# A sixth gather buffer, and value tiles in the weights' ring, in a hybrid decoder step on one core

## The chip, the cores and the metric

The kernel runs on one core of one Trainium2 chip. The metric is the device time of one execution in microseconds (us); smaller is better. A core has TensorE (PE) for matrix products, VectorE (DVE), ScalarE (ACT) and GpSimd (POOL), and a queue of SyncE (SP) from which most DMAs are issued. Each engine runs its own instructions in order and waits on semaphores for the others.

## What is computed

One inference step of a two-layer decoder for 512 prompt tokens and 8 sampled tokens. Layer 0 is a chunked gMLP, layer 1 differential attention over shared keys and values. After each of them comes a PEER layer: 8 heads pick 16 of 16384 experts for every token.

```python
def peer_block(h, w_q, keys, u_tab, v_tab):
    q = (h @ w_q).reshape(T, PEER_HEADS, 2, PEER_QDIM // 2)
    s = jnp.einsum('thcd,hcnd->thcn', q, keys)
    sv, si = lax.top_k(s, PEER_TOPK)
    cand = sv[:, :, 0, :, None] + sv[:, :, 1, None, :]
    ...
    eidx = ...                                   # 128 experts for a token
    g = jax.nn.softmax(top_s, axis=-1)
    act = jax.nn.gelu(jnp.einsum('thkd,td->thk', u_tab[eidx], h))
    return jnp.einsum('thk,thkd->td', (g * act), v_tab[eidx])
```

Tables u and v have 16384 rows of 1024 float32 in each layer. The prompt is four tiles of 128 tokens (0 to 3); the sampled tokens are tile 4.

## The kernel before

In each layer two of the four prompt tiles get their experts by gathers and two by dense products over the whole tables (`DT`: tiles 0 and 1 dense in layer 0, tiles 2 and 3 in layer 1).

**Gathers** (`peer_tile`, lines 710 to 723): for each tile 128 rows of u and 128 of v for every token, each by an indirect DMA from POOL (`gather`, line 706) that brings 128 rows of 1024 float32 into a buffer of the pool `gb`, which has 5. DVE then multiplies a gathered u row tile by the tokens and sums (line 715), or adds a weighted v row tile to the residual x (line 722). There are 512 gathers in a layer. They need little else and are laid beside the rest of the kernel: `pins` and `anchors` allow each of these DVE operations only behind a certain instruction of the other work (`tick`).

**Dense experts** (`dense_peer`): the 128 blocks of 128 experts are done in four quarters q of 32 blocks il. `acts(q)` loads a tile of u (`ub`, line 483, 512 KB) from the ring `wt`, which the pool `wp` keeps with 4 buffers for all weights. In quarter 0 it is multiplied by float32 matmuls (line 494). In the others `split` makes a high part (ACT, line 209) and a low part (DVE, line 211), with two buffers each, and 24 matmuls follow (lines 488, 489, 491); ACT writes the gelu into `W[q]`. `gates(q)` builds one-hot tiles (ACT, lines 526 and 529, or DVE, line 520), multiplies them on PE (line 533) and applies the gates to `W[q]`. The value loop (lines 552 to 586) loads a tile of v (`vb`, line 561, 512 KB) for each block and accumulates W x v into four PSUM banks (line 576, or with split operands in quarter 3, lines 572 to 574).

In program order, quarter 0's activations come first, then quarter 0's gates with quarter 1's activations. In the value loop of quarter q each of the first four value tiles (`NV` = 4) is followed by 8 activations of quarter q + 1, where those aren't done yet (q = 1 and 2); the other 28 are interleaved with the gates of quarter q + 1. Value tiles of quarter 3 come from the ring `wt`, all others from a ring `vb` of three in the pool `dpa`. The Tile framework orders the instructions of each engine when it compiles: an instruction that comes first in the program goes first if what it needs, a buffer among it, is free by then; otherwise later ones pass it.

**Fronts**: ahead of the dense experts of each layer stand the gMLP or the attention, for two groups of tiles, and `peer_front`, which makes queries and scores (ACT copies a score tile, line 650) and has DVE pick the top 16 (`topk_rank`). For the first group of a layer the scores go to a ring `s_k` of two in the pool `wk`, for the second to memory of its own (`sall`), and for the sampled tokens to `s_k` again (line 680).

Of the kernel before, what the change touches and what calls it, by code (L numbers as in the profile page):

```python
# [8 lines left out]
F32 = mybir.dt.float32  # L9
# [9 lines left out]
D = 1024  # L19
# [16 lines left out]
def body(ctx: ExitStack, tc: tile.TileContext, a):  # L36
# [1 line left out]
    V, SC, PE, GP, SY = nc.vector, nc.scalar, nc.tensor, nc.gpsimd, nc.sync  # L38

    per = ctx.enter_context(tc.tile_pool(name="per", bufs=1))  # L40
    gb = ctx.enter_context(tc.tile_pool(name="gb", bufs=5))
    ks = ctx.enter_context(tc.tile_pool(name="ks", bufs=2))
    wp = ctx.enter_context(tc.tile_pool(name="wp", bufs=4))
    pt = ctx.enter_context(tc.tile_pool(name="pt", bufs=4, space=bass.MemoryType.PSUM))
# [43 lines left out]
    def step(k=1):  # L88
        while k and bg:
            try:  # L90
                next(bg[0])
                k -= 1
            except StopIteration:
                bg.pop(0)
# [48 lines left out]
    def bcast_row(src, n, name, bufs=2, p=128):  # L143
        t = wk.tile([128, n], F32, name=name, tag="tmp" if n == D else f"bc{n}", bufs=1)
        SY.dma_start(t[:p], bass.AP(tensor=src.tensor, offset=src.offset, ap=[[0, p], [1, n]]))
        return t
# [60 lines left out]
    def split(w, k=1):  # L207
        wh = wp.tile([128, 8, 128], FR, name="wh", tag="wh", bufs=2)
        SC.activation(wh, w, AF.Copy)  # L209
        wl = wp.tile([128, 8, 128], FR, name="wl", tag="wl", bufs=2)  # L210
        tick(V.tensor_tensor(wl, w, wh.bitcast(F32), op=OP.subtract), k)  # L211
        return wh, wl
# [256 lines left out]
    def dense_peer(layer, dpa, open_rest, open_odd, smp):  # L469
# [3 lines left out]
        NQ, QI, NV = 4, 32, 4  # L473
# [78 lines left out]
        for q in range(NQ):  # L552
            na, ng = (na if not q else acts(q + 1), gates(q + 1)) if q + 1 < NQ else (iter(()), iter(()))
            for il in range(QI):
                i = q * QI + il
                w = W[q][:, il, :]
                r0 = layer * NE + i * 128
                three = q in V3[layer] and (il >= NV or q == NQ - 1)
                v = wp.tile([128, D], F32, name="vb", tag="wt") if three else \
                    dpa.tile([128, D], F32, name="vb", tag="vb", bufs=3)  # L560
                SY.dma_start(v, a["peer_v"][r0:r0 + 128, :])
                if three:
                    vh, vl = [z.rearrange("p c e -> p (c e)") for z in split(v.rearrange("p (c e) -> p c e", c=8), 0)]
                    wh = dpb.tile([128, 256], FR, name="wdh", tag="ohj", bufs=4)
                    SC.activation(wh, w, AF.Copy)
                    wl = dpb.tile([128, 256], FR, name="wdl", tag="ohj", bufs=4)
                    V.tensor_tensor(wl, w, wh.bitcast(F32), op=OP.subtract)
                for t in range(2):
                    for hf in range(2):
                        ts, hs = slice(t * 128, (t + 1) * 128), slice(hf * 512, (hf + 1) * 512)  # L570
                        if three:
                            PE.matmul(y[t][hf], wh[:, ts], vh[:, hs], start=i == 0, stop=False)
                            PE.matmul(y[t][hf], wh[:, ts], vl[:, hs], start=False, stop=False)  # L573
                            PE.matmul(y[t][hf], wl[:, ts], vh[:, hs], start=False, stop=i == 127)
                        else:
                            PE.matmul(y[t][hf], w[:, ts], v[:, hs], start=i == 0, stop=i == 127)  # L576
                if i == 2:
                    bg.append(peer_sample(layer, dpa, *smp))
                if il % 2 == 0:
                    step(1)  # L580
                if il < NV:
                    for _ in range(QI // NV):
                        next(na, None)
                else:
                    for _ in range((il - NV + 1) * 16 // (QI - NV) - (il - NV) * 16 // (QI - NV)):
                        next(ng, None)
# [5 lines left out]
    def peer_front(tiles, n, layer, ph):  # L592
        if any(t == 4 or t not in DT[layer] for t in tiles):
            gbc = bcast_row(a["f_norm_g"][layer], D, f"g_f{layer}")
        hT = dd["hT"] = full_T("hT")
        st = {}
        for t, r in zip(tiles, rms([(x[t], rows[t]) for t in tiles], D)):
            p = rows[t]
            if t < 4 and t not in DT[layer]:
                h = ks.tile([128, D], F32, name="h_g", tag="hg")  # L600
            elif t == 4:
                hs = ks.tile([128, D], FR, name="h_s", tag="hs", bufs=1)
                h = wa.tile([128, D], F32, name="h_s32", tag="h", bufs=HB[0])
                V.memset(h[:32], 0.0)
            else:
                norm_T(t, r, (3 + layer, hT))
                st[t] = [None]
                continue
            V.scalar_tensor_tensor(h[:p], x[t][:p], r, gbc[:p], op0=OP.mult, op1=OP.mult)
            to_T(h, rows[t], hT, col(t))  # L610
            st[t] = [h]
            if t == 4:

                SC.activation(hs[:32], h[:32], AF.Copy)
                V.tensor_tensor(hs[32:32 + NB], h[:NB], hs[:NB].bitcast(F32), op=OP.subtract)
                st[t] = [hs[:32 + NB]]
        for t in tiles:
            st[t].append(topk_state(8 if t < 4 else 1))
        if 4 in tiles:
            qz = [wa.tile([128, 8, 72], F32, name=f"qz{c}", tag="zT", bufs=ZB[0]) for c in range(2)]  # L620
            for z in qz:
                V.memset(z, 0.0)
            pss = [pm.tile([64, 128], F32, name=f"ps_ss{c}", tag="mm") for c in range(2)]

        sall = {}
        if stage[0] % 2 and 1:
            tl = [t for t in tiles if t < 4]
            for tag, m in ((("kTall", 2), ("vall", 2)) if layer else (("uv", 3),)):
                m = min(m, len(tl))
                z = ph.tile([128, m, 4, 4, 128], F32, name="s_" + tag, tag=tag)  # L630
                sall.update({tl.pop(0): z[:, k] for k in range(m)})
        for sp in range(4):
            hf, o = sp // 2, sp % 2 * 4
            if not o:
                kT = wp.tile([128, 8, 128], F32, name="keysT", tag="wt")
                SY.dma_start(kT, a["keysT"][layer][:, hf * 8:hf * 8 + 8, :])
                qT = wk.tile([128, 8, NW[0]], F32, name="qT", tag="qT", bufs=1)

            def q_out(ft, ps):
                SC.activation(qT[:, o + ft, :n], ps[:, :n], AF.Copy)  # L640

            dense(a["peer_wq"][layer], 8, hT, n, q_out, sp * 4, sp * 4 + 4, [5, 2, 4, 3][stage[0]], 3 * layer)
            for t in tiles:
                c0 = col(t)
                if t < 4:
                    s = sall[t][:, sp] if sall else wk.tile([128, 4, 128], F32, name="s_k", tag="s_k", bufs=2)
                    ps = pm.tile([128, 4, 128], F32, name="ps_s", tag="mm")
                    for i in range(4):
                        PE.matmul(ps[:, i, :], qT[:, o + i, c0:c0 + 128], kT[:, o + i, :], start=True, stop=True)
                    SC.activation(s, ps, AF.Copy)  # L650
                    bg.append(topk_rank(s.rearrange("p (h c) n -> p h c n", c=2), 128, 2, st[t][1], sp * 2))
                    if sp == 3:
                        bg.append(tile_finish(t, st[t], layer))
                else:
                    qv = qT[:, o:o + 4, col(4):col(4) + NB].rearrange("p (h c) b -> p h c b", c=2)
                    for c in range(2):
                        V.tensor_copy(qz[c][:, sp * 2:sp * 2 + 2, 0:8], qv[:, :, c, :])
                        fl = qz[c].rearrange("p h x -> p (h x)")
                        for h in range(sp * 2, sp * 2 + 2):
                            PE.matmul(pss[c], fl[:, h * 64:(h + 1) * 64], kT[:, 2 * (h % 4) + c, :],  # L660
                                      start=h == 0, stop=h == 7)
                    if sp == 3:
                        bg.append(sample_finish(pss, st[t], layer))
        return st
# [12 lines left out]

    def sample_finish(pss, st, layer):
        state = st.pop()
        s = wk.tile([64, 1, 2, 128], F32, name="s_s", tag="s_k", bufs=2)  # L680
        for c in range(2):
            SC.activation(s[:, 0, c], pss[c], AF.Copy)
        yield from topk_rank(s, 64, 1, state, 0)
# [522 lines left out]
```

## Time and profile before

| | us |
|---|---|
| median of 3 runs | 3254.13 |
| lowest and highest | 3252.62 to 3262.15 |
| profiled execution | 3267.74 |
| its span, first to last instruction | 3266.0 |

| stage, us from the span's start | what runs |
|---|---|
| 0 to 200 | layer 0: gMLP and scores of tile 2 |
| 200 to 540 | gMLP and scores of tiles 0, 1, 3 and 4, beside gathers of tile 2 |
| 540 to 690 | activations of quarter 0, top-k |
| 690 to 825 | gates of quarter 0, activations of quarter 1 |
| 825 to 980 | values of quarter 0, gates of quarter 1 |
| 980 to 1440 | quarters 1 and 2: activations, values, gates |
| 1440 to 1570 | values of quarter 3 |
| 1570 to 2310 | layer 1: keys, values, attention, scores; gathers from 1780 on |
| 2310 to 3266 | dense experts of layer 1 |

The profile is one execution, recorded by the hardware. Times inside it count from its first instruction. An engine's busy time is what its instructions take; PE's matmuls overlap, so their single durations don't add up, and their starts tell the pace. In its records a float32 matmul of line 576 counts twice, so a value tile has 8. A wait is put down to the instruction or DMA that ended it.

### The profile page before, as it was taken

The page shows a single profiled execution, that of the slowest core. Times are in us where ns is not written, and L with a number is a line of the kernel's source. Part 1 is how long each engine was busy: PE and PEld are TensorE (multiplying, and loading weights), DVE is VectorE, ACT ScalarE, POOL GpSimd, SP SyncE. Part 2 cuts the span into 40 slices and gives each one's busy share as a digit, 9 for nine tenths or more (in the row PEclk, how much of TensorE's full clock was granted, in tenths as well). Part 3 has the DMA queues.
Part 4 walks back from the last instruction along what each step waited for, and adds up shares of the span by engine and source line. Part 5 has one row for each costly group of instructions (what it writes and reads, how often), then busy time and mean ns, then how long its engine had stood idle before and what let it go on. Part 6 is the DMA issues. An engine that isn't in the chain of part 4 may idle for free.

```text
span 3266.0 us, 50065 instructions
## 1 busy us (share of the span) xinstructions
PE 2997.8 (92%) x18048; PEld 2237.3 (69%) x18048; DVE 2424.0 (74%) x5095; ACT 1382.3 (42%) x3156; POOL 1334.2 (41%) x1061
## 2 busy tenths in 40 slices
PE   7998979889899999978898988688799999999999
PEld 7898646788458758646787643455689658757757
DVE  1489779679776776679725788869989887686685
ACT  2344021256583593583353233321237433363444
POOL 0036662024555454455300556534334455354340
PEclk9999989999999999989999988699899999999999
DMA  7678987468999899889955989777778999989885
GB/s 247 230 280 308 336 318 244 149 225 304 386 345 365 319 350 373 313 306 373 351 168 189 361 311 324 253 266 239 284 275 308 340 364 361 328 314 355 329 306 165
DMA packets 271563, 976.54 MB, mean 299 GB/s; under 512 B 30938, under 2 KB 31770, under 8 KB 271306
## 3 DMA queue, kind: packets, MB, share of 16 engines
q0 software_dynamic: 152064, 553.72, 46.9%
q1 hardware_dynamic: 119250, 419.62, 36.1%
q8 instruction: 142, 2.33, 0.3%
q14 instruction: 107, 0.88, 0.1%
HBM read 966.76 MB, written 6.46 MB: 298 GB/s over the span
## 4 chain that ended last, share of the span: by engine, by line
PE 53%; DVE 13%; issue 12%; DMA 11%; POOL 7%; ACT 4%; another core or an unknown queue 0%; SPq 0%; POOLq 0%; DVEq 0%; ACTq 0%
PE y L576 13%; PE ps_d L231 7%; POOL gath L706 7%; PE ps_a L494 6%; PE ps_a L488 5%; PE ps_a L489 5%; PE ps_a L491 4%; DMA gath<-peer_v,ix 4%; DMA gath<-peer_u,ix 3%; PE ps_g L533 3%; DVE x L722 2%; ACT ohj L526 2%; DVE si L369 2%; DVE gath L715 2%; PE y L573 1%
## 5 line engine op out<-in xcount | busy, mean ns | idle before, releaser
L706 POOL DMA_INDIRECT gath<-peer_u,ix x512 | 651.5, 1272 | 947.4 <-DVE ix L674 355.5
L706 POOL DMA_INDIRECT gath<-peer_v,ix x512 | 644.8, 1259 | 718.2 <-DVE x L722 381.3
L722 DVE SCALAR_TENSOR_TENSOR x<-gath,act,x 128x1024 f32<-128x1024 f32 x512 | 655.6, 1281 | 70.3 <-DMA gath<-peer_v,ix 59.7
L576 PE MATMUL y<-vb,W 128*128 128x512 f32 x1536 | 703.4, 604 | 0.9 <-DMA vb<-peer_v 0.9
L715 DVE SCALAR_TENSOR_TENSOR gath<-gath,h_g 128x1024 f32<-128x1024 f32 x512 | 615.6, 1221 | 95.3 <-DMA gath<-peer_u,ix 94.0
L526 ACT ACTIVATE ohj<-iota,selJ 128x128 f16<-128x128 f32 x1408 | 426.0, 389 | 166.9 <-PE ps_g L533 152.8
L576 PEld LDWEIGHTS y<-vb,W 128*128 128x128 f32 x1536 | 283.3, 193 | 301.9 <-issue 299.2
L231 PE MATMUL ps_d<-hT,wt 128*128 128x128 f32 (+3 forms) x2048 | 433.6, 371 | 26.8 <-DMA wt<-w_in 5.9
L488 PE MATMUL ps_a<-hPh,wh 128*128 128x256 f32 x1536 | 399.5, 297 | 13.2 <-ACT wh L209 12.8
L231 PEld LDWEIGHTS ps_d<-hT,wt 128*128 128x128 f32 x2048 | 307.2, 200 | 139.2 <-issue 18.5
L211 DVE TENSOR_TENSOR wl<-ub,wh 128x1024 fp32r<-128x1024 f32 x192 | 234.9, 1224 | 205.3 <-ACT wh L209 177.7
L489 PE MATMUL ps_a<-hPl,wh 128*128 128x256 f32 x1536 | 382.2, 286 | 0.0
L209 ACT ACTIVATE wh<-ub 128x1024 fp32r<-128x1024 f32 x192 | 202.0, 1054 | 278.7 <-PE ps_a L489 243.5
L488 PEld LDWEIGHTS ps_a<-hPh,wh 128*128 128x128 f32 x1536 | 298.0, 194 | 26.3 <-ACT wh L209 14.3
L489 PEld LDWEIGHTS ps_a<-hPl,wh 128*128 128x128 f32 x1536 | 297.9, 194 | 8.9 <-issue 8.9
L494 PE MATMUL ps_a<-hT,ub 128*128 128x256 f32 x1024 | 228.2, 384 | 25.2 <-ACT W L499 25.2
L533 PEld LDWEIGHTS <-ohj 128*128 128x128 f16 x4096 | 182.3, 121 | 98.1 <-issue 55.9
L494 PEld LDWEIGHTS ps_a<-hT,ub 128*128 128x128 f32 x1024 | 196.1, 193 | 54.1 <-ACT W L499 26.0
L533 PE MATMUL ps_g<-gi,ohj 128*128 128x32 f16 x4096 | 193.0, 205 | 42.1 <-ACT ohj L529 24.6
L491 PE MATMUL ps_a<-hPh,wl 128*128 128x256 f32 x1536 | 224.4, 289 | 2.0 <-DVE wl L211 2.0
L499 ACT ACTIVATE W<-ps_a 128x256 f32<-128x256 f32 x256 | 96.0, 378 | 306.1 <-PE ps_a L491 149.3
L491 PEld LDWEIGHTS ps_a<-hPh,wl 128*128 128x128 f32 x1536 | 200.5, 193 | 9.6 <-issue 7.0
(299 smaller groups left out, 3841.9 us busy)
## 6 DMA issues: line engine op xcount, KB each, us to landing
ub<-peer_ut SPq DMA_DIRECT2D x256, 512.0 KB
vb<-peer_v SPq DMA_DIRECT2D x256, 512.0 KB
wt<-w_in SPq DMA_DIRECT2D x64, 512.0 KB
wt<-peer_wq SPq DMA_DIRECT2D x64, 512.0 KB
wt<-w_out SPq DMA_DIRECT2D x32, 512.0 KB
gath<-peer_u,ix POOLq DMA_INDIRECT x512
gath<-peer_v,ix POOLq DMA_INDIRECT x512
wt<-w_k SPq DMA_DIRECT2D x16, 512.0 KB
```

Of the source, the lines that this page charges most:

```text
L211: tick(V.tensor_tensor(wl, w, wh.bitcast(F32), op=OP.subtract), k)
L231: z = PE.matmul(ps[:, :n], wt[:, c, :], rhs[:, c0 + c, :n], start=c0 + c == 0, stop=c0 + c == nk - 1)
L488: PE.matmul(ps, uh[:, c, :], hP[0][:, c, :], start=c == 0, stop=False)
L489: PE.matmul(ps, uh[:, c, :], hP[1][:, c, :], start=False, stop=False)
L491: PE.matmul(ps, ul[:, c, :], hP[0][:, c, :], start=False, stop=c == 7)
L494: z = PE.matmul(ps, u[:, c, :], hT[:, c, :256], start=c == 0, stop=c == 7)
L526: SC.activation(oh[:, :, k], iota128, AF.Abs, scale=-1.0, bias=selJ[:, t2 + k:t2 + k + 1])
L533: PE.matmul(ps[:, :, t - t1], oh[:, :, k], gi[:, c, (t - t0) // 2, :, t % 2], start=c == 0, stop=c == 1)
L576: PE.matmul(y[t][hf], w[:, ts], v[:, hs], start=i == 0, stop=i == 127)
L706: GP.indirect_dma_start(out=t, out_offset=None, in_=table, in_offset=bass.IndirectOffsetOnAxis(ap=ix[:, k:k + 1], axis=0))
L715: z = V.scalar_tensor_tensor(u, u, 1.0, h, op0=OP.mult, op1=OP.mult, accum_out=act[:, k:k + 1])
L722: z = V.scalar_tensor_tensor(x[t], v, act[:, k:k + 1], x[t], op0=OP.mult, op1=OP.add)
```

## The change

The pool of gather buffers grows from 5 to 6. The ring `vb` goes from three buffers to one and is used only for il 0 to 3 of quarters 1 and 2; all other value tiles come from the ring `wt` (before, only quarter 3's). The ring `s_k` has one buffer in layer 0 instead of two, in layer 1 two as before. Nothing is computed otherwise.

```diff
-    gb = ctx.enter_context(tc.tile_pool(name="gb", bufs=5))
+    gb = ctx.enter_context(tc.tile_pool(name="gb", bufs=6))
...
                 three = q in V3[layer] and (il >= NV or q == NQ - 1)
-                v = wp.tile([128, D], F32, name="vb", tag="wt") if three else \
-                    dpa.tile([128, D], F32, name="vb", tag="vb", bufs=3)
+
+                v = wp.tile([128, D], F32, name="vb", tag="wt") if il >= NV or q in (0, NQ - 1) else \
+                    dpa.tile([128, D], F32, name="vb", tag="vb", bufs=1)
                 SY.dma_start(v, a["peer_v"][r0:r0 + 128, :])
...
-                    s = sall[t][:, sp] if sall else wk.tile([128, 4, 128], F32, name="s_k", tag="s_k", bufs=2)
+                    s = sall[t][:, sp] if sall else wk.tile([128, 4, 128], F32, name="s_k", tag="s_k", bufs=1 + layer)
...
-        s = wk.tile([64, 1, 2, 128], F32, name="s_s", tag="s_k", bufs=2)
+        s = wk.tile([64, 1, 2, 128], F32, name="s_s", tag="s_k", bufs=1 + layer)
```

## Rows read from the trace of the kernel before

**Rows 1.** The page's head: span; busy time, share and instructions of each engine.
```profile
span 3266.0 us, 50065 instructions
PE 2997.8 (92%) x18048; PEld 2237.3 (69%) x18048; DVE 2424.0 (74%) x5095; ACT 1382.3 (42%) x3156; POOL 1334.2 (41%) x1061
```

**Rows 2.** Stages: us; busy PE, PEld, DVE, ACT, POOL; PE clock, DMA share, GB/s.
```profile
200.00:500.00 300.00, 268.55 (x1224) 210.21 (x1223) 246.20 (x436) 79.11 (x144) 188.01 (x140) 0.94 0.90 327
...
690.00:825.00 135.00, 123.82 (x1244) 116.62 (x1243) 124.17 (x158) 97.71 (x223) 67.51 (x49) 0.97 0.85 295
825.00:980.00 155.00, 144.77 (x860) 76.11 (x859) 115.46 (x175) 105.24 (x287) 85.39 (x74) 0.96 0.97 367
980.00:1120.00 140.00, 140.00 (x993) 118.42 (x993) 94.51 (x110) 51.31 (x92) 63.95 (x49) 1.00 0.94 348
1120.00:1210.00 90.00, 84.90 (x594) 43.38 (x593) 68.11 (x90) 90.00 (x247) 46.98 (x38) 1.00 0.92 338
...
1440.00:1570.00 130.00, 104.08 (x480) 79.80 (x480) 117.63 (x152) 57.50 (x102) 70.21 (x55) 0.90 0.91 339
...
1780.00:2170.00 390.00, 328.65 (x1101) 180.96 (x1100) 305.13 (x593) 128.34 (x294) 218.18 (x170) 0.85 0.85 302
2170.00:2320.00 150.00, 125.17 (x448) 78.37 (x446) 132.71 (x602) 15.96 (x32) 60.66 (x52) 0.91 0.76 270
```

**Rows 3.** Waits of DVE from 200 to 500: us in total, times, longest.
```profile
DVE gath L715 <- DMA gath<-peer_u,ix: 24.4, 25, 4.5
DVE x L722 <- DMA gath<-peer_v,ix: 20.2, 21, 2.6
```

**Rows 4.** Waits of DVE from 1780 to 2170.
```profile
DVE gath L715 <- DMA gath<-peer_u,ix: 35.9, 27, 6.8
DVE x L722 <- DMA gath<-peer_v,ix: 11.6, 11, 2.7
```

**Rows 5.** Waits of POOL over the whole span.
```profile
POOL gath L706 <- DVE x L722: 511.0, 237, 15.9
```

**Rows 6.** Chain that ended last, 360 to 425: start us, us, what.
```profile
379.78 8.78 DMA gath<-peer_v,ix
...
388.65 1.29 DVE x L722
...
402.56 7.41 DMA gath<-peer_v,ix
```

**Rows 7.** Timeline of SP's queue: start us, us, line, issue, tiles, count.
```profile
984.96 21.05 SPq L483 DMA_DIRECT2D ub<-peer_ut  x7
1008.84 0.33 SPq L561 DMA_DIRECT2D vb<-peer_v  x1
```

**Rows 8.** Records of line 576 by stage: us; busy PE, PEld; clock, DMA, GB/s.
```profile
690.00:825.00 135.00, 9.02 (x21) 4.03 (x22) 0.97 0.85 295
...
980.00:1120.00 140.00, 39.98 (x90) 16.17 (x90) 1.00 0.94 348
```

**Rows 9.** Timeline of PE: last third of three activations, a value tile behind the second.
```profile
2966.25 1.12 PE L491 MATMUL ps_a<-hPh,wl 128*128 128x256 f32 x8
2969.13 1.12 PE L491 MATMUL ps_a<-hPh,wl 128*128 128x256 f32 x8
...
2975.44 1.12 PE L491 MATMUL ps_a<-hPh,wl 128*128 128x256 f32 x8
```

**Rows 10.** The stretch around rows 9, columns as in rows 2.
```profile
2960.00:2980.00 20.00, 20.00 (x149) 18.08 (x148) 15.29 (x15) 8.11 (x12) 7.55 (x7) 1.00 0.97 367
```

**Rows 11.** Waits of PE from 690 to 825.
```profile
PE ps_a L488 <- ACT wh L209: 8.8, 4, 3.4
```

**Rows 12.** Waits of PE over the whole span.
```profile
PE y L576 <- DMA vb<-peer_v: 0.9, 2, 0.5
```

**Rows 13.** Timeline of DVE and ACT: last read of a score tile, next copy.
```profile
146.47 0.29 DVE L369 FIND_INDEX8 si<-sv,s_k 128x8 uint32<-128x128 f32 x1
...
149.08 0.60 ACT L650 ACTIVATE s_k<-ps_s 128x512 f32<-128x512 f32 x1 [0.17 <-PE ps_s L649]
```

## The prediction

> **What bounds the kernel now.** I read the page's top first: the span is 3266.0 us and PE is busy 92% of it [rows 1], so only what PE leaves idle, or spends at the lower clock, can be won. Next comes the table by stage, which tells where that is [rows 2]. There are two kinds of stage. In the dense expert stages PE has little left: it is busy 140.00 of 140 us at 980 to 1120, 144.77 of 155 at 825 to 980. In the stages ahead of them it has much more: 268.55 of 300 at 200 to 500, 328.65 of 390 at a granted clock of 0.85 (part of it at 1.2 GHz) at 1780 to 2170, 125.17 of 150 at 2170 to 2320, and 104.08 of 130 at the seam of the two layers.
>
> What holds PE in these stages is VectorE's queue, which runs in order and carries the gathered rows between the operations that PE needs. At 200 to 500 it is busy 246.20 us and waits 24.4 + 20.2 = 44.6 us for gathered rows, 97% of the stage together [rows 2, 3]. At 1780 to 2170 it is busy 305.13 us and waits 35.9 + 11.6 = 47.5 us [rows 2, 4]. What follows in the queue (softmax scalars, norms, top-k) is late by these waits. The waits by POOL tell why the rows are late: POOL stood 511.0 us for VectorE to hand back a buffer after line 722 alone [rows 5]. The ring is full nearly always. One trip round it is a flight of 7.41 to 8.78 us from issue to landing and 1.29 us of VectorE [rows 6], 8.7 to 10.1 us, over five buffers 1.7 to 2.0 us a gather before any waiting for POOL's or VectorE's turn. Measured are 300 / 140 = 2.14 and 390 / 170 = 2.29, by POOL's counts [rows 2]. So the ring's depth sets the pace there.
>
> **The sixth gather buffer.** It adds no instruction. With an unchanged trip the pace could be 2.14 x 5 / 6 = 1.8 us, enough to end all these waits; against that stands the DMA traffic, 0.90 of the engines' time at 200 to 500. The highest long rate in the table is 367 GB/s (825 to 980). At 1780 to 2170 ending the waits needs 302 x 390 / 342.5 = 344 GB/s, which fits; the bounds are 0 and 47.5 us, and I take the middle, 24, because a sixth request also lengthens the queue in which the other five stand. At 200 to 500 ending them would need 327 x 300 / 255.4 = 384 GB/s, which doesn't fit; at 367 the gain is at most 300 - 300 x 327 / 367 = 33 us. Half is 16, and as PE is idle only 31.5 of these 300 us I count two thirds, 11. At 2170 to 2320 VectorE's whole idle time is 150 - 132.71 = 17.3 us, at 1440 to 1570 it is 12.4 [rows 2], and gathers have but a share of it: 4 and 3, a quarter each. Sum 42 us saved, bounds 0 and 47.5 + 33 + 17.3 + 12.4 = 110. What is late next in these stages is VectorE's own work (82% and 78% busy now).
>
> The limit matters. In this trace the DMA engines hold 367 GB/s for 155 us [rows 2]. The Trainium skill, "DMA: Bandwidth & Descriptors", section "Where 436 GB/s comes from", puts what HBM gives one core at about 358 GB/s; by that the term at 200 to 500 would be 300 - 300 x 327 / 358 = 26, halved and cut to two thirds 9 instead of 11, and the sum 40. The measured rate is the higher, and I keep it.
>
> **The value tiles.** Today they have a ring of three and the u tiles (later the activations' weights) a ring of four. So SP can load both kinds at once, and the scheduler mixes them: at 985 to 1009 seven u loads are followed by a value load, and so on [rows 7]; at 980 to 1120 line 576 has 90 records, 8 to a tile, so 11 value tiles run between 32 activations [rows 8]. After the change the values from il 4 on stand in the same ring behind all 32 u tiles of the next activations. Only the four with a buffer of their own can run between them. So PE gets first 32 activations with 4 values, then 28 values with the gates.
>
> The cost is whether PE stays full in the first part. An activation takes PE 2969.13 - 2966.25 = 2.88 us, a value tile 2975.44 - 2969.13 - 2.88 = 3.43 us [rows 9]. The part has 32 x 2.88 + 4 x 3.43 = 106 us of PE work and 36 loads. The nearest row is 2960 to 2980, where some six activations and one value ran [rows 9, 10], nearly this mix, and PE was busy 20.00 of 20 us, with VectorE at 15.29 and DMA at 0.97 [rows 10]. It says nothing is lost; but the DMA engines are then at their end, and a row that comes late delays the split, behind which PE stands. The other end is 690 to 825, activations and gates with hardly any values: PE 123.82 of 135 us, 8.8 us of it waiting for the split's first half [rows 2, 11], 8.3% idle, 9 us in a part of 106. There are four such parts (quarters 1 and 2 of two layers). I take 3 each, nearer to the first row since its mix is the closer: +12, bounds 0 and 36.
>
> At 690 to 825 itself 21 records, 2.6 value tiles, ran early out of their own ring [rows 8]; after the change they can't. That moves 2.6 x 3.43 = 9 us of filler; bounds 0 and 9, I take 4, in two layers +8. The other way: at 1120 to 1210 ScalarE is busy 90.00 of 90 us and PE 84.90 [rows 2], since eleven values have gone ahead and the gates' one-hots have too little PE work beside them. With 28 values there it is 96 us of PE work more evenly laid beside them; 5.1 us idle here, about twice in layer 0; I take -5, bounds 0 and -10.
>
> Seams, from values back to activations: the first u tile now waits until value 28 gives its slot back. Then PE still has values 29 to 31 and the next quarter's first, 4 x 3.43 = 13.7 us; a flight of 8.8 us [rows 6] and a split, which keeps up with 2.88 us an activation, make 11.7. Hidden, 0; without that cover up to 11.7 at each of four seams. One value buffer instead of three between activations: its reload has eight activations, 23 us, for a flight of 8.8. Hidden as well; while SP waits at that load for PE, the u loads behind it wait too, but four u tiles are ahead. A ring of four instead of three where only values run: PE waited 0.9 us in all for values [rows 12]; at most -1, counted 0.
>
> **The score buffer** in layer 0: its last reader ends at 146.76, and the next copy starts at 149.08 [rows 13]; the other two hand-overs of layer 0 have more room. 0; the sampled token's copy, late in the layer, has nobody to wait for. If VectorE fell 2.3 us behind, ScalarE and the next query copies would wait by the same.
>
> Sum: -42 + 12 + 8 - 5 = -27 us. The profiled execution took 3267.74 us, 13.6 above the median of 3254.13; it would be 3241, and the median **3227 us**.
>
> **Rivals.** A, slower: taking the values out from between the activations costs more than the gathers give. Its place is the four activation parts, its mechanism VectorE's in-order queue: a late row delays the split, and PE has no value tile in between. Price by the far row: 36 + 2 x 9 = 54, and as gathers then crowd with back-to-back u loads I leave half of their gain, 21: 3254 + 33 = 3287. It decides from 106 + 10 = 116 us for such a part on. Against it speaks the stretch at 2960; for it the DMA share of 0.94 at 980 to 1120 already [rows 2].
> The Trainium skill, "Perfetto Trace Analysis", section "Optimization Strategy", says that stages bound by different engines may gain from being interleaved; this change takes such an interleaving apart. By that rule rival A is the case; the rows at 980 to 1120 (PE full) agree with the rule, and the one at 2960 says that little is left to lose.
>
> B, no change: the DMA engines and not the ring are the limit, the sixth request only stands in line, and flights grow from 8 to 9.6 us at the same pace. Then only the stage at 0.85 gains, some 10 us, and 12 + 8 - 5 = 15 are lost: 3259. For it: 0.90 at 200 to 500. Against: 0.97 is reached elsewhere.
>
> C, more: the attention's whole 47.5 and the 33 come off the path, nothing is lost to the order: 3254 - 80 + 10 = 3184.
>
> That the change doesn't do what it says (the planned order of VectorE holds the pace, not the ring) is part of B: the order is made anew, each row planned behind an anchor, and the full ring [rows 5] speaks against it.
>
> **How the numbers follow.** Forecast 0.48, C 0.07, B 0.20, A 0.25. A measurement here tells about 0.3%, 10 us, from no change. Faster by more than that: 0.48 + 0.07 = 0.55; within: 0.20; slower: 0.25. The range runs from C's edge, 3188, to A's, 3288; the forecast's own is 3188 to 3244.
>
> **What would show it.** Right: in 200 to 500 and in the attention, VectorE's waits for gathered rows halved, a gather in about 2.0 us, GB/s up; the activation parts at 106 to 112 us with PE over 95%. Wrong: flights of over 9.5 us with the pace unchanged (B); PE waiting for the split at lines 488 to 491 in parts of over 116 us (A); u loads on the path at the seams.

## The result, and the profile after

The changed kernel takes 3281.43 us (median; 3275.25 to 3287.33), the kernel before beside it 3257.03: ratio 1.0076, 95% interval 1.0052 to 1.0100. It is slower by about 24 us, where 27 us less were forecast. The profiled execution took 3277.2 us with a span of 3275.5. That of the kernel before was 10.7 us above its median, so the two profiles lie only 9.5 us apart; keep that in mind with every difference of spans below.

The page's head of the kernel after (columns as in [rows 1]):

```profile
span 3275.5 us, 50108 instructions
PE 2992.1 (91%) x18048; PEld 2234.1 (68%) x18048; DVE 2421.4 (74%) x5095; ACT 1383.1 (42%) x3156; POOL 1390.0 (42%) x1061
```

The work is the same; PE is idle longer. Where, a cut of the span into four shows. The marks are the first record of quarter 0's activations and the last record of line 572 (573 after), the first matmuls of a value in quarter 3, in each layer's trace:

| us | front, layer 0 | dense, layer 0 | front, layer 1 | dense, layer 1 |
|---|---|---|---|---|
| before | 553.8 | 1011.5 | 717.8 | 975.6 |
| after | 546.4 | 1020.4 | 683.5 | 1018.0 |
| difference | -7.4 | +8.9 | -34.3 | +42.4 |

So the fronts gained 41.7 us and the dense expert stages lost 51.3. First the gain. Windows of the kernel after, columns as in [rows 2], the second one from the first gather of layer 1 on, with the like window of the kernel before under it (170 gathers in each); line numbers behind 556 are one higher than before:

```profile
200.00:500.00 300.00, 275.85 (x1270) 216.39 (x1269) 253.38 (x461) 81.95 (x150) 198.24 (x145) 0.95 0.91 337
...
1777.00:2130.00 353.00, 306.41 (x1042) 167.98 (x1040) 287.57 (x559) 117.15 (x267) 216.39 (x170) 0.88 0.91 334
```
```profile
1788.00:2170.00 382.00, 320.65 (x1076) 176.22 (x1076) 297.82 (x577) 127.36 (x292) 218.11 (x170) 0.85 0.86 307
```

Waits of DVE in the first of these windows, then in the second, both of the kernel after (us in total, times, longest), to be laid beside [rows 3, 4]:

```profile
DVE gath L716 <- DMA gath<-peer_u,ix: 16.2, 16, 4.0
DVE x L723 <- DMA gath<-peer_v,ix: 12.7, 15, 2.5
```
```profile
DVE gath L716 <- DMA gath<-peer_u,ix: 26.6, 22, 7.6
...
DVE x L723 <- DMA gath<-peer_v,ix: 1.8, 2, 1.4
```

The waits for gathered rows fell from 44.6 to 28.9 us and from 47.5 to 28.4; POOL's wait for line 722's buffers fell from 511.0 [rows 5] to 448.8, and a gather takes 300 / 145 = 2.07 us at 200 to 500 instead of 2.14, and 353 / 170 = 2.08 in layer 1 instead of 382 / 170 = 2.25.

That isn't the whole gain, though. In layer 1 a part of it lies ahead of every gather of that layer. Layer 0's last gather and layer 1's first attention score, first in the kernel before (whose mark at the end of layer 0's dense experts lies at 1565.4), then in the kernel after (1566.8):

```profile
1616.24 1.01 POOL L706 DMA_INDIRECT gath<-peer_v,ix  x1 [0.30 <-issue]
1642.48 0.48 PE L898 MATMUL ps_sc<-kTall,qTa 64*128 64x128 f32 x2
```
```profile
1547.07 0.94 POOL L707 DMA_INDIRECT gath<-peer_v,ix  x1 [0.59 <-DVE x L723]
1631.14 0.49 PE L899 MATMUL ps_sc<-kTall,qTa 64*128 64x128 f32 x2
```

In the kernel before 20 gathers of layer 0 were left over when its dense experts ended; in the kernel after there are none. From the mark to the first score it is 77.1 us before and 64.3 after, so 12.8 of layer 1's 34.3 us are won there. Now the loss. Waits of PE over the whole span, first the kernel before, then the kernel after:

```profile
PE ps_a L488 <- ACT wh L209: 12.8, 6, 3.4
...
PE y L573 <- DVE wl L211: 11.4, 7, 5.8
...
PE y L572 <- ACT wh L209: 3.7, 3, 1.2
```
```profile
PE ps_a L488 <- ACT wh L209: 60.3, 40, 5.3
...
PE y L573 <- ACT wh L209: 18.8, 15, 1.7
...
PE y L574 <- DVE wl L211: 0.8, 2, 0.5
```

Line 488 is the first matmul of an activation, line 209 the first half of the split of its weight tile, on ScalarE. PE waits 47.5 us longer for it. (The last quarter's values waited 3.7 us for ScalarE's half of the split and 11.4 for VectorE's, lines 572 and 573; these are 573 and 574 after the change, with 18.8 and 0.8, so 4.5 us more in all.) PE waits so in the four activation parts of quarters 2 and 3, where 32 activations now run with three to four value tiles between them (windows, columns as in [rows 2], and the wait of PE in each):

```profile
978.00:1103.00 125.00, 117.45 (x907) 108.98 (x907) 97.63 (x103) 54.19 (x99) 71.46 (x53) 0.99 0.95 363
1218.00:1338.00 120.00, 107.17 (x833) 98.83 (x832) 95.05 (x100) 41.25 (x65) 72.24 (x50) 1.00 0.97 365
2680.00:2812.00 132.00, 121.45 (x927) 113.09 (x925) 103.15 (x125) 48.18 (x83) 78.75 (x58) 0.98 0.97 364
2935.00:3060.00 125.00, 107.99 (x810) 98.80 (x810) 94.88 (x111) 41.07 (x64) 72.35 (x49) 1.00 0.95 357
```
```profile
PE ps_a L488 <- ACT wh L209: 7.1, 5, 1.4
PE ps_a L488 <- ACT wh L209: 12.8, 9, 1.5
PE ps_a L488 <- ACT wh L209: 8.5, 6, 1.4
PE ps_a L488 <- ACT wh L209: 17.0, 12, 1.4
```

That is 32 waits and 45.4 us, 1.42 each. The DMA engines are at 0.95 to 0.97 there, and it would be easy to call them the cause. The timelines of ScalarE and of PE around one such wait say something else (start, us, engine, line, tiles, in brackets the idle time before and its releaser):

```profile
2944.95 0.38 ACT L499 ACTIVATE W<-ps_a 128x256 f32<-128x256 f32 x1 [2.49 <-PE ps_a L491]
2945.23 2.00 ACT L209 ACTIVATE wh<-ub 128x1024 fp32r<-128x1024 f32 x2
```
```profile
2943.79 1.12 PE L491 MATMUL ps_a<-hPh,wl 128*128 128x256 f32 x8
2946.33 0.39 PE L488 MATMUL ps_a<-hPh,wh 128*128 128x256 f32 x1 [1.42 <-ACT wh L209]
```

ScalarE was idle for 2.49 us, and what ended that was not a tile's landing but PE's end of activation k. It stood before the gelu copy of activation k (line 499, 0.38 us). The split of the tile of k+1 (line 209, 1.05 us) stands behind that copy in ScalarE's queue, though it needs nothing of it. So the next activation starts 0.38 + 1.05 = 1.43 us after the last one ended. In the kernel before PE shows no wait of this kind in the four parts. Of their 124 pairs of neighbouring activations 96 have no value tile between them, and in all of these the split stands ahead of the copy. It stands behind in only 5 pairs, each with two to three value tiles (3.43 us of PE apiece) between.

### The profile page after: what moved, and what is told of

It reads as the page before. It is cut to its first block, busy times and chain, and to the rows that moved or that the text cites. A ratio compares the mean times of both kernels' runs of the same rounds, so it can differ in the third digit from the quotient of the medians.

```text
span 3275.5 us, 50108 instructions
## 1 busy us (share of the span) xinstructions
PE 2992.1 (91%) x18048; PEld 2234.1 (68%) x18048; DVE 2421.4 (74%) x5095; ACT 1383.1 (42%) x3156; POOL 1390.0 (42%) x1061
## 3 DMA queue, kind: packets, MB, share of 16 engines
q0 software_dynamic: 152064, 553.72, 45.8%
## 4 chain that ended last, share of the span: by engine, by line
PE 74%; DVE 11%; ACT 6%; DMA 5%; issue 3%; POOL 1%; SPq 0%; DVEq 0%; ACTq 0%; POOLq 0%
PE y L577 20%; PE ps_d L231 14%; PE ps_a L494 6%; PE ps_a L488 5%; PE ps_a L489 5%; PE ps_a L491 5%; PE ps_g L533 4%; DVE gath L716 2%; ACT wh L209 2%; PE y L574 2%; DMA gath<-peer_v,ix 2%; ACT ohj L526 2%; DVE si L369 2%; PE y L575 2%; DVE x L723 1%
## 5 line engine op out<-in xcount | busy, mean ns | idle before, releaser
L707 POOL DMA_INDIRECT gath<-peer_u,ix x512 | 683.2, 1334 | 926.2 <-DVE ix L675 414.6
L707 POOL DMA_INDIRECT gath<-peer_v,ix x512 | 664.0, 1297 | 591.8 <-DVE x L723 294.0
L577 PE MATMUL y<-vb,W 128*128 128x512 f32 x1536 | 696.0, 599 | 0.0
L723 DVE SCALAR_TENSOR_TENSOR x<-gath,act,x 128x1024 f32<-128x1024 f32 x512 | 655.2, 1280 | 34.3 <-DMA gath<-peer_v,ix 28.4
L488 PE MATMUL ps_a<-hPh,wh 128*128 128x256 f32 x1536 | 398.3, 296 | 60.3 <-ACT wh L209 60.3
L231 PEld LDWEIGHTS ps_d<-hT,wt 128*128 128x128 f32 x2048 | 305.5, 200 | 135.9 <-issue 15.8
L209 ACT ACTIVATE wh<-ub 128x1024 fp32r<-128x1024 f32 x192 | 198.9, 1051 | 64.3 <-PE ps_a L489 45.1
```

Source lines behind the costliest of these rows:

```text
L231: z = PE.matmul(ps[:, :n], wt[:, c, :], rhs[:, c0 + c, :n], start=c0 + c == 0, stop=c0 + c == nk - 1)
L488: PE.matmul(ps, uh[:, c, :], hP[0][:, c, :], start=c == 0, stop=False)
L707: GP.indirect_dma_start(out=t, out_offset=None, in_=table, in_offset=bass.IndirectOffsetOnAxis(ap=ix[:, k:k + 1], axis=0))
L723: z = V.scalar_tensor_tensor(x[t], v, act[:, k:k + 1], x[t], op0=OP.mult, op1=OP.add)
```

## The experiments

**The score buffer alone.**

```
-    s = ... wk.tile([128, 4, 128], F32, name="s_k", tag="s_k", bufs=2)
+    s = ... wk.tile([128, 4, 128], F32, name="s_k", tag="s_k", bufs=1 + layer)
```

> The kernel before with one score buffer in layer 0 instead of two, nothing else. T and the prediction: within 5 us of before, 3252 to 3262. Rival: if the copies of scores stand behind the top-k, the first front is 5 to 10 us longer.

3259.19 us, ratio 1.0003 (0.9990 to 1.0016). The score buffer costs nothing.

**The sixth buffer without the ring's change.** To make room for it the value tiles keep a ring of their own, but of two; the score buffer as above.

```
-    gb = ... bufs=5
+    gb = ... bufs=6
-        dpa.tile([128, D], F32, name="vb", tag="vb", bufs=3)
+        dpa.tile([128, D], F32, name="vb", tag="vb", bufs=2)
```

> The sixth gather buffer without the weights' ring: gb 6, value tiles in a ring of their own as before, but of two buffers instead of three to make room, score buffer as in the change. Theory T (the gathers gain, the shared ring loses): the fronts end as early as in the changed kernel, 7 us in layer 0 and 34 in layer 1, the dense stages take what they took before plus at most 5 for the shorter value ring; 3215 to 3225 us. Rival R1 (denser gathers crowd the dense stages, whatever ring the values have): the dense stages of layer 1 lose 30 to 40 us again; 3255 to 3275.

3371.05 us, ratio 1.0351 (1.0330 to 1.0373): a miss for both. What the run lacked was a control for the ring of two.

**The ring of two alone**, five gather buffers (of the edits above only the value ring's).

> The kernel before with the value tiles' own ring of two instead of three, all else as before (five gather buffers). It is what the run of the sixth buffer alone gave up to make room. Theory P (the ring of two was the price in that run, 3371): 3370 to 3420, the dense stages longer by 50 to 85 us each, since the fronts' gain of some 35 us of the sixth buffer is missing here. Rival G (denser gathers cost the interleaved order that much): this kernel stays at 3257 to 3290.

3374.70 us, ratio 1.0341 (1.0310 to 1.0372): theory P. The value matmuls of this run, what PE's weight loads and matmuls together waited for (us, times), and the waits of PE over the span:

```profile
  DMA vb<-peer_v: 124.3, 82
```
```profile
PE y L576 <- DMA vb<-peer_v: 51.7, 38, 3.9
```

The second was 0.9 in [rows 12], the first 3.6 in the same view of the kernel before. The whole 118 us are the price of the third value buffer, and the run of the sixth buffer alone says nothing on the sixth buffer: beside this one it gained 3.7 us, within what these runs can tell.

**The ring's change alone**: the value tiles as in the change, five gather buffers, two score buffers.

> Only the values' move into the weights' ring (one buffer of their own), five gather buffers and two score buffers as before. T: no gain in the fronts, the loss of about 50 us in the dense stages stays; 3295 to 3310. R1: without the sixth buffer nothing crowds; 3250 to 3265.

3268.32 us, ratio 1.0038 (1.0021 to 1.0056), between the two ranges and so a miss for both. The ring costs some 11 us, and the sixth buffer on top of it, meant to be the gain, another 13. In the parts PE waited for the split here as well, 4 + 4 + 3 + 3 = 14 times, 20.0 us; last part:

```profile
PE ps_a L488 <- ACT wh L209: 4.3, 3, 1.4
```

Counting ScalarE's records shows why the numbers differ. In the kernel after, 6, 12, 7 and 13 splits of the four parts stand behind the copy of the activation ahead of them, 38 in all; in the ring alone 6, 5, 3 and 4, 18; in the kernel before 1, 1, 1 and 2 (the first split of a part isn't counted). Not every one costs a wait (32 of the 38 do), since five have a value tile ahead of them.

**The copy written later**: the changed kernel with the gelu copy of activation k put, in the program, behind the split of k+1.

```
     uh, ul = split(u, ...)
+    if il:
+        SC.activation(W[q][:, il - 1, :], last, AF.Gelu_apprx_tanh)
+    last = ps
...
-    SC.activation(W[q][:, il, :], ps, AF.Gelu_apprx_tanh)
+    if not q or il == QI - 1:
+        SC.activation(W[q][:, il, :], ps, AF.Gelu_apprx_tanh)
```

> The changed kernel, with the gelu copy of activation k written one activation later in the program, behind the split of activation k + 1 (quarters 1 to 3). T (PE's repeated 1.42 us waits in the activation parts come from ScalarE's order: it stands at the copy of activation k, which waits for PE, while the next split is behind it): 32 such waits of 1.42 us vanish, the parts shrink from 119 to 132 us to 106 to 112; 3281 - 45 = 3230 to 3250. Rival R2 (the u loads can't keep up out of a ring of four that also serves the values): the waits stay and only change their name; 3270 to 3285.

3283.26 us, ratio 1.0081 (1.0061 to 1.0100), PE's wait for the split 60.5 us. At first this seemed to acquit ScalarE. But in its trace the same 38 splits stand behind their copies, at the same places: moving a line in the program hadn't moved the instruction. The experiment didn't do what it was meant to.

**The order laid down**: as above, and a dependency that only orders; the last two lines of the diff are in the split.

```
     uh, ul = split(u, ...)
+    if il:
+        z = SC.activation(W[q][:, il - 1, :], last, AF.Gelu_apprx_tanh)
+        tc.add_manual_dep(z.ins, dd["wh"], NOSYNC, reason="order")
+    last = ps
...
-    SC.activation(wh, w, AF.Copy)
+    dd["wh"] = SC.activation(wh, w, AF.Copy).ins.name
```

> The changed kernel, with one order laid down by hand: on ScalarE the gelu copy of activation k stands behind the split of the weight tile of activation k+1 (quarters 1 to 3 of both layers). In the trace of the changed kernel TensorE waits 32 times in its four activation parts for that split, 1.42 us each (0.38 us of the copy and 1.05 us of the split, both of which begin only when activation k has ended), 45 us in all; before there was none. Theory S (ScalarE's order): these waits go, the parts fall from 125, 120, 132 and 125 us to 106 to 114 each, and the time falls by 35 to 48 us from the changed kernel's 3281, to 3233 to 3248. Rival D (the DMA engines are the limit; in the parts they are busy 0.95 to 0.97): the wait only moves to the tiles, u or value, the parts stay within 4 us of what they were, and the time is 3270 to 3285.

3233.98 us, ratio 0.9935 (0.9918 to 0.9952): 47 us under the changed kernel, where theory S wanted 35 to 48. From the first matmul of its first activation to the end of its last one the four parts take 123.8, 106.6, 120.5 and 106.0 us (in the kernel after 125.0, 118.5, 131.9 and 123.9), so two of them miss theory S's 106 to 114. No split but the first of a part stands behind a copy. Windows of three of these parts, then PE's wait over the whole span (line 492 there is line 488 of the kernel after):

```profile
977.00:1100.00 123.00, 118.40 (x906) 110.63 (x904) 96.33 (x101) 54.95 (x100) 68.54 (x54) 0.97 0.95 369
1217.00:1323.00 106.00, 103.62 (x802) 96.76 (x801) 94.01 (x98) 41.05 (x62) 68.95 (x48) 1.00 1.01 399
...
2907.00:3013.00 106.00, 104.35 (x804) 97.50 (x803) 92.71 (x109) 41.11 (x63) 68.66 (x48) 1.00 1.02 406
```
```profile
PE ps_a L492 <- ACT wh L209: 15.9, 10, 5.3
```

The wait fell by 60.3 - 15.9 = 44.4 us and the span by 45.8. (The wait for VectorE's half of these splits rose meanwhile from 7.3 to 14.3 us over the span.) Rival D falls: the DMA engines moved 399 and 406 GB/s in the parts where they had moved 365 and 357. The first part alone kept its length (125.0 to 123.8); there the split's other half, on VectorE, came late instead, 4.6 us.

**The same order with five gather buffers.**

> The value tiles through the weights' ring with five gather buffers and the score buffer of two, as in the run of the ring alone, with the same order on ScalarE as the run beside it. The ring alone had 14 such waits of 1.42 us in the four parts, 20 us. Theory S: the time falls by 12 to 22 us from the ring alone's 3268, to 3246 to 3256, and stands above the run with six buffers by the gain of the sixth in the two fronts (some 50 to 60 us) less what denser gathers still cost in the dense stages. Rival D: 3262 to 3272.

3249.71 us, ratio 0.9978 (0.9967 to 0.9990), 19 under the ring alone: theory S. With this order the sixth buffer is worth 15.7 us; without it, it cost 13.

**The same order in the kernel before.**

> The kernel before with the first order alone (split of the tile of activation k+1 ahead of the gelu copy of activation k). There TensorE waits nowhere in the four activation parts, since a value's matmuls lie between the activations. Theory S: the order is worth nothing there, 3249 to 3262. If the order is worth something by itself, whatever lies between the activations: under 3245, and then the changed kernel with the order has to be set against this one.

3252.08 us, ratio 0.9990 (0.9974 to 1.0006): nothing. So the 47 us are no gain that the kernel before could have had as well. For the reason given ahead of the run it is a weak test: the order could move only the 5 splits that stood behind their copies there, all of them with value tiles between and without a wait. Everywhere else the planner had this order already.

**A like order in the last quarter's values.** There a copy of the gated activations (0.42 us) stands ahead of the split of a value tile.

```
-    SC.activation(wh, w, AF.Copy)
+    z = SC.activation(wh, w, AF.Copy)
+    tc.add_manual_dep(z.ins, dd["wh"], NOSYNC, reason="order")
```

> The changed kernel with the split ahead of the gelu copy (as in the run of that order) and the like order in the last quarter's values: ScalarE's copy of the gated activations of value i (0.42 us) stands behind the split of value i's tile, where before it could stand ahead of it. In the run with the first order alone TensorE still waits 15 times in layer 0's last quarter for that split, 17.3 us, and the stretch takes 116 us (102 with five buffers, 110.5 in the kernel before). Theory S (ScalarE's order): these waits go as well, the stretch falls to 98 to 104, the time to 3214 to 3223. Rival V (VectorE limits that stretch; it is busy 103.4 of its 116 us): the wait moves to VectorE's half of the split, the stretch stays at 112 or more, the time at 3229 to 3237.

3232.17 us, ratio 0.9923 (0.9907 to 0.9938): in the median nothing beside 3233.98, though its runs spread from 3218.86 to 3236.61. In the trace, of the fastest of these runs (3218.86), both theories have a part. Layer 0's last quarter fell from 116.0 to 104.2 us, the wait for ScalarE's half of the split is gone there, and VectorE's half has become 10.2 us:

```profile
PE y L580 <- DVE wl L211: 10.2, 15, 1.0
```

What the second order is worth stays open. This is the fastest kernel here, no faster for certain than the one with the first order alone.

**Both orders, five gather buffers.**

> The same two orders with the value tiles through the weights' ring and five gather buffers. In the run with the first order alone TensorE waits 6 times in layer 0's last quarter, 7.3 us. Theory S: 3241 to 3246, so the sixth buffer is worth 20 to 30 us to the other run of this job. Rival V: 3247 to 3253; and if denser gathers cost the dense stages by crowding, not by order, the two runs stand less than 15 us apart.

3249.02 us, ratio 0.9978 (0.9961 to 0.9995): 0.7 under the first order alone, so theory S missed here, and the second order again shows nothing in the median. The sixth buffer is worth 16.9 us in this pair. The fronts gained 4.2 + 47.5 between the two profiles (their spans are 31.4 us apart, the medians only 16.9), the dense stages gave back 13.2 + 7.0; in the pair with the first order alone 9.1 + 32.0 against 28.7 + 0.5. So the dense stages are some 20 to 30 us longer with six buffers even with the order laid down. A part of that is moved work: with five buffers 29 gathers of layer 0 are left for layer 1's front in either pair, with six none. How much of the rest is crowding at the DMA engines and how much VectorE's queue wasn't separated.

## Why the prediction was wrong

**What was right, and what of it was luck.** The sixth buffer: 42 us were forecast for the fronts, 41.7 came. That close a sum is partly luck. Layer 0's front was to gain 11 and gained 7.4. For layer 1's front 24 + 4 were counted, and 3 for the seam of the layers. Ahead of its first score 12.8 us came, behind it 34.3 - 12.8 = 21.5. What was won at the seam is the end of layer 0's left-over gathers, which the sum did not name. A shorter front needs no sixth buffer for that: in the run of the ring of two alone the dense stage of layer 0 is so long that no gather is left over, and layer 1's front is 20 us shorter than in the kernel before. The marks: the waits for gathered rows were to be halved and fell by 35% and 40%; a gather was to take about 2.0 us and takes 2.07 and 2.08. GB/s rose from 327 to 337 and from 307 to 334. So a fifth more buffers gave 3% and 8% more pace, and the ring's depth is not all that sets it.

The score buffer: 0, and its own run says 0. The seams between quarters: 0 where quarter 3's activations begin. The next quarter's first value followed the last one within 0.5 us, at 1215.6 and 2932.7, and the activations came right behind it, at 1218.6 and 2935.7. (The other two seams fall into the gates' hole, below.) One value buffer between activations: PE doesn't wait for it. The reordering itself came as described, 32 activations with three to four values and then the others with the gates.

**The step that failed** is the cost of the four activation parts, put at +3 each, with bounds of 0 and 9 for a part. The waits came to 45.4 / 4 = 11.3, beyond the far bound. The value was chosen by nearness of mix: 2960 to 2980, six activations and a value, PE 20.00 of 20 [rows 10]. But those 20 us showed places where the split stood ahead of the copy. What they couldn't show is the order the planner would choose once the values were gone, and that order was the cost: with it laid down quarter 3's parts take 106.6 and 106.0 us, against the 106 worked out from [rows 9]. (Quarter 2's hold some 14 us of other work of PE: 118.40 and 104.35 us busy in the windows of that run.) The far row, 690 to 825, had PE waiting for the same line [rows 11], but for another reason, and the prediction read it as a price without asking what stood ahead of the split in ScalarE's queue. There no split stands behind the copy of the activation ahead of it; each of the four waits follows a run of ScalarE's one-hots for the gates. The longest one (kernel before, ScalarE and then PE):

```profile
744.67 4.79 ACT L526 ACTIVATE ohj<-iota,selJ 128x128 f16<-128x128 f32 x16
...
750.32 1.04 ACT L209 ACTIVATE wh<-ub 128x1024 fp32r<-128x1024 f32 x1
```
```profile
751.41 0.39 PE L488 MATMUL ps_a<-hPh,wh 128*128 128x256 f32 x1 [3.36 <-ACT wh L209]
```

So no row of the kernel before shows the wait that decided. In the sum, the dense stages lost 51.3 us where 12 + 8 - 5 = 15 were forecast: 36 of the 51 us between the forecast and the medians. The other 15 are the two profiled executions, one 10.7 us above its median and one 4.2 below.

**Rival A** had the place and the sign: the parts took 125.0, 118.5, 131.9 and 123.9 us, all past its point of 116, and its time of 3287 is near the 3281.43 measured. Its mechanism was wrong. It blamed VectorE's queue and a late row; in the timeline it is ScalarE's queue and a copy that waits for PE, and that is shown by the run in which this order alone is changed. The Trainium skill, "Perfetto Trace Analysis", section "Optimization Strategy", on interleaving stages bound by different engines, is borne out by the kernel as built (the interleaving taken apart cost 11 us with five buffers). With the order laid down no such gain shows: 3249.71 taken apart against 3252.08 in the kernel before with the same order.

**Rival B** put the limit at the DMA engines. Its mark, flights of over 9.5 us at an unchanged pace, did not come: the gathers came faster, and 406 GB/s in a part is past every rate the prediction reckoned with. But flights did grow. Gathers of u and v rows with the median from issue to landing (us, of those whose landing the trace has), in the kernel after, then in the ring alone with five buffers:

```profile
gath<-peer_u,ix POOLq DMA_INDIRECT x512, 7.7
gath<-peer_v,ix POOLq DMA_INDIRECT x512, 7.4
```
```profile
gath<-peer_u,ix POOLq DMA_INDIRECT x512, 7.0
gath<-peer_v,ix POOLq DMA_INDIRECT x512, 7.0
```

So a part of what the sixth buffer could give went into flights 0.4 to 0.7 us longer.

**Terms off in size.** Quarter 1's activations with quarter 0's gates were to lose 4 in each layer; from the first matmul to the end of the last they lost 1.6 and 1.9 (149.5 to 151.1 us, 135.9 to 137.8). The relief of the later gates came: PE's waits for ScalarE's one-hots in the gates of quarters 2 and 3 of layer 0, 4.2 and 19.1 us before, are gone. What the sum lacked lies between the two. The values of quarter 0 now run ahead of quarter 1's gates and end early, which leaves gates alone, and PE waits there for the one-hots, 13.1 us in layer 0 and 4.9 in layer 1, where it waited for none before. From the start of quarter 1's activations to that of quarter 2's the layers lost 9.1 and 4.4 us. Layer 0 in the kernel after, just before this hole and in it:

```profile
816.00:950.00 134.00, 133.62 (x662) 65.26 (x661) 99.97 (x152) 68.69 (x190) 80.84 (x68) 1.00 1.00 394
...
950.00:978.00 28.00, 15.32 (x177) 14.42 (x178) 21.55 (x37) 28.00 (x75) 16.45 (x14) 0.55 0.86 309
```

**What stays open**: why the planner put 38 splits behind copies with six gather buffers and 18 with five. That it did is counted from the records; which of its planned times made it so wasn't tried.

## What to carry to other kernels

When a change takes filler from between the steps of a chain, don't count on the order of the instructions around it: the planner makes it anew. Look in the trace after at each helper engine's queue. Where what prepares step k+1 stands behind what finishes step k, and nothing lies between, the price is the sum of both operations for every such step, here 1.42 us. A row of the kernel before can't show it if the order was still the other way there, and a wait of the same name in another row may have another cause. A line moved in the program need not move the instruction: lay the order down and count it in the records of the run before reading anything from its time.

## What the runs showed of the hardware

The DMA engines held 399 and 406 GB/s over 106 us with six gather buffers and the order laid down; the prediction had taken 367 as the highest long rate. The figure for what HBM gives a core in the Trainium skill, "DMA: Bandwidth & Descriptors", section "Where 436 GB/s comes from", about 358 GB/s, is passed by both; here one core ran.

In the hole at 950 to 978 the granted clock was 0.55, next to the lower of its two levels (1.2 GHz), with PE busy 15.32 of 28 us, right after 134 us at 1.00 with PE busy 133.62. ScalarE's one-hots set that stretch, busy 28.00 of 28 us, and PE waited for them 13.1 us; what the lower clock cost beside that wasn't separated.
